# LayerNorm weight and bias for the next residual: applied in place by VectorE in pieces beside the next sublayer, instead of by GpSimd at the sublayer boundary

## The chip, the cores and the metric

The program runs on one core of one Trainium2 chip. The metric is device time of one execution in microseconds (us). The kernel before takes 1333.25 us as the median of three runs (1328.18 to 1336.28 us).

## The reference: what is computed

A decoder trunk of two layers over 256 tokens of width 1024, in float32. Each layer has three sublayers: a SwiGLU feed-forward (FFN), a mixer of four attention branches, and a second FFN. Every sublayer ends in the same way, and this is what the change touches:

```python
x = _layer_norm(DEEPNORM_ALPHA * x + (1 + gate) * F(x * (1 + scale) + shift), ln_g, ln_b)
# _layer_norm(r, g, b) = (r - mean) * rsqrt(var + eps) * g + b
```

The result x is needed twice. The next sublayer's matrix products need it modulated and transposed at once. The residual of the next sublayer needs it as plain rows, much later, at that sublayer's end.

## The kernel before, in words

Tokens lie in two tiles of 128 (t = 0, 1), the 1024 channels along the free axis. All products are made as three passes of exact parts (hi and lo of the weight, uh and ul of the input). A weight is loaded by SyncE's queue into one of five `raw` buffers (line 256), ScalarE rounds it to `hi` (line 259), VectorE makes `lo` = raw - hi (line 264), and only then is the `raw` buffer free for the next load. The six sublayers follow each other as FFN, mixer, FFN, FFN, mixer, FFN, so there are five boundaries between sublayers; the sixth ends the program through `store`.

**At a boundary** (`boundary`, lines 388 to 490), for each token tile: `resid` (lines 398 to 400) takes the products out of PSUM times the gate row G, adds ALPHA x, and gathers the statistics; `stats` (403 to 405) makes rstd, whose power is GpSimd's (405); `xhat` (413 or 415) normalizes the rows in four pieces of 256 columns; `norm` (423 to 434) transposes each piece on TensorE, scales and shifts it (429 on ScalarE or 431 on VectorE), and splits it into uh (433, ScalarE) and ul (434, VectorE). The LayerNorm weight and bias of the modulated input are folded into the column vectors gd and bd (383 to 385). Tile 0 goes through this while TensorE still makes the last products of the old sublayer; tile 1 goes through it in `finish`, behind the products of tile 0 in the new one.

**The rows for the next residual** are made in `rest` (480 to 488): four pairs on GpSimd, times the row g (486) and plus the row b (487), from the normalized rows `rt` into a new tile `x`. They are queued behind the boundary's last instructions on their engine.

**The rows g, b and G** of a sublayer come by GpSimd: a memset (345), a small load issued by GpSimd (346), and later a shuffle on VectorE that spreads the row over the partitions (352). Three buffers of the tag `row` hold them; a new row waits until the old row of its buffer is read. `sub_steps` says beside which of twelve steps of the sublayer each fetch is issued (ROW_G = 3, ROW_B = 4, GG = 4); the steps themselves are pairs of loads of adaLN weights and a multiply-and-sum on VectorE (304, 305).

**Order.** The program is written in one order with priorities, and a scheduler then orders each engine's queue by its own estimate of when things are ready; `high_priority` moves pieces ahead. In the mixer, `plan` lists which piece of attention follows which half pair of projections (a tick); `rope` (677 to 680) ends in an add on GpSimd (680) that the attention scores (875) wait for. In the FFN, `hidden(f)` is one pair of column tiles of the first product, and `post` (524 to 534) its activation; TensorE needs its PSUM bank back when VectorE has made `h` (527). The first two column tiles of an FFN are made per token tile, and `hT` (611) transposes their result, which waits for `h` (609).

Of the kernel before, what the change touches and what calls it, by code (L numbers as in the profile page):

```python
# [11 lines left out]
F32 = mybir.dt.float32  # L12
F32R = mybir.dt.float32r
BF16 = mybir.dt.bfloat16
AF = mybir.ActivationFunctionType
# [18 lines left out]
# columns of mix_w_in  # L34
# [5 lines left out]
# pairs of 128-column tiles whose products come out transposed  # L40
# [7 lines left out]
# offsets in the constants  # L48
C_COS, C_SIN, C_END = 0, 256, 512
# offsets in the constants of sums  # L50
R_ONE, R_SUF, R_FOX = 0, 128, 256
R_END = 256 + 640
# offsets in the masks
C_MC, C_MT, C_MA = 0, 384, 768
M_END = 768 + 1152
# depths of buffers, priorities and places of the pieces of work among each other
# [48 lines left out]
PJ = 5  # L105


def _consts():
# [5 lines left out]
    # minus sums of the first and of the second key tile, by columns (q0 k0, q1 k0, q1 k1)  # L114
# [27 lines left out]
def trunk(ctx: ExitStack, tc: tile.TileContext, x, xT, crow, ada0, adac, adab, w_in0, w_in0x, gcol, bcol, ln_g, ln_b,  # L142
# [46 lines left out]
    # 2 silu(c) = c * (1 + tanh(c / 2))  # L189
# [43 lines left out]
    held = {"ins": [], "left": 0, "free": 0}  # L233

    def behind():
        """queue what follows behind the boundary that has just been emitted, on its engines."""
        stack = ExitStack()
        for i in held["ins"]:
            stack.enter_context(tc.issue_after(i))
        return stack  # L240
# [4 lines left out]
    def load(*srcs):  # L245
        """srcs: [128, n] each; the parts of their halves, which are loaded in turns."""
# [32 lines left out]
    def split_mm(ps, w, xh, xl, start, stop, w_stationary=True):  # L279
        """ps += w^T x by three passes of exact parts."""  # L280
# [11 lines left out]
    mods = {(l, s): {} for l in range(DEPTH) for s in range(3)}  # L292

    def ada_cols(l, s, v):
        """steps that leave sum_k cond_k W_kn + b_n (+ 1) in columns [128, n // 128]."""
# [14 lines left out]
    def ada_gate(l, s):  # L310
        """steps that leave sum_k cond_k W_kn + b_n + 1 in every row of G."""
# [19 lines left out]
    def modulate(src, uh, ul, gd, bd, on_act):  # L331
        """parts of src * gd + bd; src may lie in PSUM."""
# [9 lines left out]
    def fetch_row(dst, row):  # L342
        """a row of DRAM into one partition of each 32; spread_row spreads it from there."""
# [16 lines left out]
    def sub_steps(l, s, nxt):  # L360
        """steps beside a sublayer's products: its gate and its LayerNorm's rows, the modulation of what follows."""
# [8 lines left out]
        for key, n, src in (("g", ROW_G, ln_g), ("b", ROW_B, ln_b)):  # L370
# [4 lines left out]
        seq = ada_cols(l, s, 2) + nx  # L375
        return [both(*before.get(n, []), f) for n, f in enumerate(seq)]

# [10 lines left out]
    def boundary(rt, accs, i, G, g, b, u, nxt):  # L388
        """rows: r = ALPHA x + G O, then LayerNorm; into u: its modulation for what follows."""
# [106 lines left out]
    def ffn(l, s, u, nxt, steps, first=False):  # L496
# [117 lines left out]
        for f in range(f0, NF):  # L614
            hidden(f)
            if first and f == F0 + SI:
                small_inputs()
# [562 lines left out]
```

## Time and profile before

| what | value |
|---|---|
| runs | 1328.18, 1333.25, 1336.28 us |
| profiled execution: its span, first to last instruction | 1336.7 us |
| TensorE busy | 1279.5 us (96%) |
| VectorE busy | 1045.9 us (78%) |
| ScalarE busy | 655.5 us (49%) |
| GpSimd busy | 193.0 us (14%) |
| read from HBM | 297.81 MB, 224 GB/s over the span |

The profile gives the profiled execution by its span alone; the span is 0.3% above the median of the three runs and 0.03% above the longest of them. The five boundaries lie near 207, 471, 671, 872 and 1134 us after the start. A row of the timeline gives start, duration, engine, line, operation, the tile written and the tiles read, and in brackets how long the engine was idle before it and which instruction ended that idle time.

### The profile page before, as it was taken

The page shows a single profiled execution, that of the slowest core. Times are in us where ns is not written, and L with a number is a line of the kernel's source. Part 1 is how long each engine was busy: PE and PEld are TensorE (multiplying, and loading weights), DVE is VectorE, ACT ScalarE, POOL GpSimd, SP SyncE. Part 2 cuts the span into 40 slices and gives each one's busy share as a digit, 9 for nine tenths or more (in the row PEclk, how much of TensorE's full clock was granted, in tenths as well). Part 3 has the DMA queues.
Part 4 walks back from the last instruction along what each step waited for, and adds up shares of the span by engine and source line. Part 5 has one row for each costly group of instructions (what it writes and reads, how often), then busy time and mean ns, then how long its engine had stood idle before and what let it go on. Part 6 is the DMA issues. An engine that isn't in the chain of part 4 may idle for free.

```text
span 1336.7 us, 23420 instructions
## 1 busy us (share of the span) xinstructions
PE 1279.5 (96%) x9178; PEld 1185.8 (89%) x9178; DVE 1045.9 (78%) x1661; ACT 655.5 (49%) x1023; POOL 193.0 (14%) x190
## 2 busy tenths in 40 slices
PE   6999998999999999999989999989999999899997
PEld 6989987899989889998979998988999998899996
DVE  7787888999855898876698876698997658986565
ACT  4644355457754445534345434354567544454440
POOL 0130004305011040000040000052060110400000
PEclk9999999999999989999999999989999999999999
DMA  9888992767755539877439877437677554596540
GB/s 340 317 294 317 314 312 95 254 193 254 254 177 188 190 132 319 307 265 248 149 138 315 301 266 243 140 126 248 201 252 242 189 190 158 174 328 199 184 142 32
DMA packets 85846, 300.41 MB, mean 225 GB/s; under 512 B 10604, under 2 KB 12316, under 8 KB 85736
## 3 DMA queue, kind: packets, MB, share of 16 engines
q1 hardware_dynamic: 84392, 298.00, 65.7%
q8 instruction: 72, 1.18, 0.3%
q10 hardware_dynamic: 576, 0.60, 0.1%
q0 software_dynamic: 768, 0.32, 0.1%
q14 instruction: 38, 0.31, 0.1%
HBM read 297.81 MB, written 1.07 MB: 224 GB/s over the span
## 4 chain that ended last, share of the span: by engine, by line
PE 57%; DMA 17%; DVE 16%; issue 5%; ACT 4%; POOL 1%; SPq 0%; DVEq 0%; ACTq 0%; POOLq 0%
PE mm L283 12%; PE mm L284 11%; PE mm L285 11%; DMA raw<-in_w_in_dram 10%; DVE lo L264 6%; DMA raw<-in_adac_dram 6%; PE acc L289 5%; PE acc L287 5%; PE acc L288 5%; DVE raw L305 2%; ACT hi L259 2%; DVE rt L415 2%; PE tp L283 1%; PE tp L284 1%; PE tp L285 1%
## 5 line engine op out<-in xcount | busy, mean ns | idle before, releaser
L264 DVE TENSOR_TENSOR lo<-raw,hi 128x1024 fp32r<-128x1024 f32 (+2 forms) x421 | 509.6, 1223 | 178.9 <-ACT hi L259 176.1
L259 ACT CAST hi<-raw 128x1024 fp32r<-128x1024 f32 (+1 forms) x422 | 434.6, 1040 | 354.6 <-PE mm L284 133.9
L283 PE MATMUL mm<-uh,hi 128*128 128x256 f32 x2032 | 576.8, 284 | 6.4 <-DVE h L527 5.4
L284 PE MATMUL mm<-ul,hi 128*128 128x256 f32 x2032 | 573.2, 282 | 0.0
L285 PE MATMUL mm<-uh,lo 128*128 128x256 f32 x2032 | 572.5, 282 | 0.3 <-DVE lo L264 0.3
L283 PEld LDWEIGHTS mm<-uh,hi 128*128 128x128 f32 x2032 | 385.0, 190 | 13.9 <-issue 6.3
L284 PEld LDWEIGHTS mm<-ul,hi 128*128 128x128 f32 x2032 | 385.1, 190 | 1.4
L285 PEld LDWEIGHTS mm<-uh,lo 128*128 128x128 f32 x2032 | 385.0, 190 | 0.8 <-DVE lo L264 0.5
L305 DVE CUSTOM_DVE_ANT_0 raw<-raw,cond_row,adab 128x1024 f32<-128x1024 f32 x128 | 164.1, 1292 | 43.2 <-DMA raw<-in_adac_dram 43.0
L287 PE MATMUL acc<-hi,hh 128*128 128x512 f32 x352 | 140.6, 399 | 1.7 <-ACT hh L533 1.6
L288 PE MATMUL acc<-lo,hh 128*128 128x512 f32 x352 | 139.1, 395 | 0.0
L289 PE MATMUL acc<-hi,hl 128*128 128x512 f32 x352 | 138.3, 396 | 0.4 <-POOL hl L534 0.4
L289 PEld LDWEIGHTS acc<-hi,hl 128*128 128x128 f32 x352 | 66.0, 188 | 17.8 <-DVE hl L534 1.2
L533 ACT CAST hh<-h 128x256 fp32r<-128x256 f32 x82 | 33.2, 405 | 98.7 <-DVE h L527 96.9
L287 PEld LDWEIGHTS acc<-hi,hh 128*128 128x128 f32 x352 | 66.1, 188 | 17.0 <-ACT hh L533 3.3
L405 POOL TENSOR_TENSOR rstd<-rstd,nhalf 128x1 f32<-128x1 f32 x12 | 7.6, 633 | 494.7 <-DVE rstd L404 494.7
L288 PEld LDWEIGHTS acc<-lo,hh 128*128 128x128 f32 x352 | 66.1, 188 | 13.9
L1065 POOL TENSOR_TENSOR merged<-merged,tg 128x512 f32<-128x512 f32 x16 | 23.0, 1451 | 143.8 <-DVE tg L1063 97.1
L289 PE MATMUL acc<-hi,ul 128*128 128x256 f32 (+1 forms) x128 | 41.3, 323 | 2.2 <-DVE ul L434 2.2
L287 PE MATMUL acc<-hi,uh 128*128 128x256 f32 (+1 forms) x128 | 41.7, 326 | 0.0
L534 DVE TENSOR_TENSOR hl<-h,hh 128x256 fp32r<-128x256 f32 x74 | 31.1, 420 | 12.6 <-ACT hh L533 12.6
L288 PE MATMUL acc<-lo,uh 128*128 128x256 f32 (+1 forms) x128 | 40.5, 316 | 0.0
(242 smaller groups left out, 1583.8 us busy)
## 6 DMA issues: line engine op xcount, KB each, us to landing
raw<-in_w_in_dram SPq DMA_DIRECT2D x174, 512.0 KB, 5.6
raw<-in_adac_dram SPq DMA_DIRECT2D x128, 512.0 KB, 5.4
raw<-in_mpair_dram SPq DMA_DIRECT2D x104, 512.0 KB, 5.1
raw<-in_w_out_dram SPq DMA_DIRECT2D x88, 512.0 KB, 5.4
ada<-in_ada_dram SPq DMA_DIRECT2D x16, 512.0 KB, 6.7
raw<-in_mwo_dram SPq DMA_DIRECT2D x16, 512.0 KB, 4.1
raw<-in_mv_dram SPq DMA_DIRECT2D x16, 384.0 KB, 3.5
raw<-in_mbr_dram SPq DMA_DIRECT2D x12, 512.0 KB, 3.9
```

The source lines that it names most:

```text
L259: nc.scalar.copy(hi[:, :half], raw[:, :half])
L264: held["lo"] = nc.vector.tensor_sub(lo[:, :half], raw[:, :half], hi[:, :half].bitcast(F32)).ins
L283: nc.tensor.matmul(ps, lhsT=wh, rhs=xh, start=start, stop=False)
L284: nc.tensor.matmul(ps, lhsT=wh, rhs=xl, start=False, stop=False)
L285: nc.tensor.matmul(ps, lhsT=wl, rhs=xh, start=False, stop=stop)
L287: nc.tensor.matmul(ps, lhsT=xh, rhs=wh, start=start, stop=False)
L288: nc.tensor.matmul(ps, lhsT=xh, rhs=wl, start=False, stop=False)
L289: return nc.tensor.matmul(ps, lhsT=xl, rhs=wh, start=False, stop=stop).ins
L305: nc.vector.tensor_tensor_reduce(raw, raw, cond_row, 0.5, adab_sb[:, l * 3 + s, v, n:n + 1], ALU.mult, ALU.add, accum_out=t[:, n:n + 1])
L415: nc.vector.tensor_scalar(rt[:, t, hs], rt[:, t, hs], mv[t][:, 0:1], rstd[t], op0=ALU.subtract, op1=ALU.mult)
L533: nc.scalar.copy(hh, h)
L534: eng.tensor_sub(hl, h, hh.bitcast(F32))
```

## The change

`rest` goes. The residual sum is now written into the tile x itself (line 399 before, 402 now), xhat, transposes and `store` work on x, and no new tile is made. The weight and bias are applied to x in place by VectorE, by `affine(t, h)`, in four pieces of two instructions (lines 485 and 486 now), one piece for each token tile and half of the columns. The pieces are handed to the next sublayer: an FFN emits one after each `hidden(f)` from f = 3 on, a mixer emits them at ticks 42 to 45. In the mixer the rows g and b are fetched at step 10 instead of 3 and 4, and two empty steps are added so that their spreading still comes three steps later. Constants, comments and line numbers apart, this is the diff:

```diff
+AFF = 3
+AM = 42
+ROW_M = 10
...
-        for key, n, src in (("g", ROW_G, ln_g), ("b", ROW_B, ln_b)):
+        for key, n, src in (("g", ROW_M if s == 1 else ROW_G, ln_g), ("b", ROW_M if s == 1 else ROW_B, ln_b)):
...
-        seq = ada_cols(l, s, 2) + nx
+        seq = ada_cols(l, s, 2) + nx + ([lambda: None] * (ROW_M + GD + 1 - 12) if s == 1 else [])
...
-            nc.vector.scalar_tensor_tensor(rt[:, t, c], xt[t][:, c], ALPHA, rt[:, t, c], op0=ALU.mult, op1=ALU.add)
-            nc.vector.bn_stats(st6[:, 2 * t + h], rt[:, t, c])
+            nc.vector.scalar_tensor_tensor(xt[t][:, c], xt[t][:, c], ALPHA, rt[:, t, c], op0=ALU.mult, op1=ALU.add)
+            nc.vector.bn_stats(st6[:, 2 * t + h], xt[t][:, c])
...
-                nc.vector.tensor_scalar(rt[:, t, hs], rt[:, t, hs], mv[t][:, 0:1], rstd[t], op0=ALU.subtract, op1=ALU.mult)
+                nc.vector.tensor_scalar(xt[t][:, hs], xt[t][:, hs], mv[t][:, 0:1], rstd[t], op0=ALU.subtract, op1=ALU.mult)
...
-            rest()
-
-        def rest():
-            with behind():
-                for t in range(2):
-                    xn = ap_.tile([P, D], F32, tag=f"x{t}", bufs=1, name=f"x{t}")
-                    for h in range(2):
-                        hs = slice(h * 512, (h + 1) * 512)
-                        nc.gpsimd.tensor_tensor(xn[:, hs], rt[:, t, hs], g[:, hs], op=ALU.mult)
-                        nc.gpsimd.tensor_tensor(xn[:, hs], xn[:, hs], b[:, hs], op=ALU.add)
-                    xt[t] = xn
...
+        def affine(t, h):
+            hs = slice(h * 512, (h + 1) * 512)
+            nc.vector.tensor_tensor(xt[t][:, hs], xt[t][:, hs], g[:, hs], op=ALU.mult)
+            nc.vector.tensor_tensor(xt[t][:, hs], xt[t][:, hs], b[:, hs], op=ALU.add)
+
+        held.update(finish=finish, first=last["pe", 0], affine=[lambda t=t, h=h: affine(t, h) for t in range(2) for h in range(2)])
...
             hidden(f)
+            if not first and f >= AFF and held["affine"]:
+                held["affine"].pop(0)()
...
+            for n, piece in enumerate(held["affine"]):
+                on(AM + n, piece)
```

The scheduler has the last word on where the pieces stand. **VectorE at the first boundary**, from tile 1's last residual sum to its four xhat; x_108 and x_109 are the rows of token tiles 0 and 1. Before:

```order
L434 TENSOR_TENSOR ul<-utmp,uh 128x2x128
L398 TENSOR_TENSOR rt<-acc,G 128x512
L434 TENSOR_TENSOR ul<-utmp,uh 128x2x128
L399 SCALAR_TENSOR_TENSOR rt<-x_109,rt 128x512
L434 TENSOR_TENSOR ul<-utmp,uh 128x2x128
L400 BN_STATS st_2246<-rt 128x6
L403 BN_AGGR mvar<-st_2246 128x2
L404 TENSOR_SCALAR rstd<-mvar 128x1
L415 TENSOR_SCALAR rt<-rt,mvar,rstd 128x256 x4
```

The same stretch of VectorE's queue in the changed kernel, where L485 is the multiply by g and L486 the add of b:

```order
L437 TENSOR_TENSOR ul<-utmp,uh 128x2x128
L486 TENSOR_TENSOR x_108<-x_108,b 128x512
L401 TENSOR_TENSOR rt<-acc,G 128x512
L437 TENSOR_TENSOR ul<-utmp,uh 128x2x128
L402 SCALAR_TENSOR_TENSOR x_109<-x_109,rt 128x512
L437 TENSOR_TENSOR ul<-utmp,uh 128x2x128
L403 BN_STATS st_2246<-x_109 128x6
L485 TENSOR_TENSOR x_108<-x_108,g 128x512
L406 BN_AGGR mvar<-st_2246 128x2
L486 TENSOR_TENSOR x_108<-x_108,b 128x512
L407 TENSOR_SCALAR rstd<-mvar 128x1
L418 TENSOR_SCALAR x_109<-x_109,mvar,rstd 128x256 x4
```

The first piece's multiply stands a little ahead of these rows, behind tile 1's first BN_STATS. So tile 0's two pieces, four instructions, have moved ahead of tile 1's rstd and xhat; this is so at all five boundaries. Of tile 1's two pieces the first multiply stands right behind the boundary's last L437, ahead of six of the next sublayer's lo, and the other three instructions among its first products.

**GpSimd at the same boundary**, into the mixer. Before:

```order
L405 TENSOR_TENSOR rstd<-rstd,nhalf 128x1
L486 TENSOR_TENSOR x_2408<-rt,g 128x512 x2
L487 TENSOR_TENSOR x_2408<-x_2408,b 128x512 x2
L486 TENSOR_TENSOR x_2413<-rt,g 128x512 x2
L487 TENSOR_TENSOR x_2413<-x_2413,b 128x512 x2
L345 MEMSET b 128x1024
L345 MEMSET G 128x1024
L346 DMA b<-in_ln_b_dram 4x1024
L680 TENSOR_TENSOR qa<-qa,t_2508 128x256
L680 TENSOR_TENSOR qa<-qa,t_2515 128x256
L680 TENSOR_TENSOR qa<-qa,t_2583 128x256
```

And in the changed kernel:

```order
L408 TENSOR_TENSOR rstd<-rstd,nhalf 128x1
L680 TENSOR_TENSOR qa<-qa,t_2498 128x256
L680 TENSOR_TENSOR qa<-qa,t_2505 128x256
L348 MEMSET g 128x1024
L348 MEMSET b 128x1024
L349 DMA g<-in_ln_g_dram 4x1024
L349 DMA b<-in_ln_b_dram 4x1024
L680 TENSOR_TENSOR qa<-qa,t_2573 128x256
```

The eight instructions of `rest` are gone, and the fetch of g and b has moved in between two of the rope's adds. In an FFN the eight are gone too, and the fetch of g stays where it was.

**VectorE late in layer 0's second FFN**, at the last adaLN step of that FFN. Before:

```order
L525 SCALAR_TENSOR_TENSOR th<-th,mm 128x256
L305 ISA raw,scale<-raw,cond_row,adab 128x1024
L305 ISA scale 128x1
L264 TENSOR_TENSOR lo<-raw,hi 128x1024
L383 TENSOR_TENSOR gd<-gcol,scale 128x8
L384 TENSOR_TENSOR bd<-bcol,scale 128x8
L527 SCALAR_TENSOR_TENSOR h<-th,mm 128x256
```

And in the changed kernel:

```order
L523 SCALAR_TENSOR_TENSOR th<-th,mm 128x256
L308 ISA raw,scale<-raw,cond_row,adab 128x1024
L308 ISA scale 128x1
L525 SCALAR_TENSOR_TENSOR h<-th,mm 128x256
L386 TENSOR_TENSOR gd<-gcol,scale 128x8
L387 TENSOR_TENSOR bd<-bcol,scale 128x8
L267 TENSOR_TENSOR lo<-raw,hi 128x1024
```

Here h has moved ahead of a lo and of the two small products; at the same place of the next FFN the order stays as before. SyncE's queue, which issues the weight loads, is the same row for row.

## Rows read from the trace of the kernel before

**Rows 1.** The page, part 1: busy time, share of the span, instructions.

```profile
PE 1279.5 (96%) x9178; PEld 1185.8 (89%) x9178; DVE 1045.9 (78%) x1661; ACT 655.5 (49%) x1023; POOL 193.0 (14%) x190
```

**Rows 2.** The page, part 4: the chain that ended last, by engine.

```profile
PE 57%; DMA 17%; DVE 16%; issue 5%; ACT 4%; POOL 1%; SPq 0%; DVEq 0%; ACTq 0%; POOLq 0%
```

**Rows 3.** Busy time by stretch: the five boundaries, and one FFN between them.

```profile
core 0: us, PE busy (x) PEld busy (x) DVE busy (x) ACT busy (x) POOL busy (x), PEclk, DMA share, GB/s
206.70:222.40 15.70, 12.00 (x58) 10.16 (x57) 14.91 (x21) 7.56 (x17) 13.95 (x13) 0.89 0.01 2
470.50:489.00 18.50, 15.97 (x108) 14.73 (x107) 17.62 (x26) 9.08 (x18) 15.22 (x14) 0.82 0.07 19
669.00:688.00 19.00, 15.30 (x117) 13.76 (x116) 18.13 (x28) 10.39 (x21) 15.21 (x14) 1.00 0.02 6
870.00:888.00 18.00, 14.60 (x70) 12.61 (x69) 17.01 (x25) 9.73 (x21) 14.91 (x14) 0.81 0.01 2
1133.50:1151.50 18.00, 14.98 (x107) 13.90 (x106) 17.12 (x25) 9.46 (x18) 15.19 (x14) 0.91 0.05 12
...
495.00:665.00 170.00, 167.39 (x1159) 155.36 (x1158) 130.24 (x187) 76.30 (x103) 1.13 (x2) 0.99 0.77 265
```

**Rows 4.** VectorE in order of time at the first boundary.

```profile
202.47 0.73 DVE L415 TENSOR_SCALAR rt<-rt,mvar,rstd 128x256 f32<-128x256 f32 x2
...
205.68 0.43 DVE L434 TENSOR_TENSOR ul<-utmp,uh 128x256 fp32r<-128x256 f32 x1
...
206.94 0.69 DVE L398 TENSOR_TENSOR rt<-acc,G 128x512 f32<-128x512 f32 x1
207.54 0.41 DVE L434 TENSOR_TENSOR ul<-utmp,uh 128x256 fp32r<-128x256 f32 x1
...
210.61 5.18 DVE L415 TENSOR_SCALAR rt<-rt,mvar,rstd 128x256 f32<-128x256 f32 x4 [0.68 <-POOL rstd L405]
...
216.75 1.88 DVE L434 TENSOR_TENSOR ul<-utmp,uh 128x256 fp32r<-128x256 f32 x2
...
221.43 5.75 DVE L264 TENSOR_TENSOR lo<-raw,hi 128x1024 fp32r<-128x1024 f32 x5
```

**Rows 5.** GpSimd in order of time there: the first and last of `rest`.

```profile
210.55 2.54 POOL L486 TENSOR_TENSOR x<-rt,g 128x512 f32<-128x512 f32 x2
...
218.31 2.92 POOL L487 TENSOR_TENSOR x<-x,b 128x512 f32<-128x512 f32 x2
```

**Rows 6.** TensorE in order of time: tile 1's first ul product, first and second boundary.

```profile
217.26 0.69 PE L289 MATMUL acc<-hi,ul 128*128 128x384 f32 x1 [0.23 <-DVE ul L434]
...
481.32 0.58 PE L289 MATMUL acc<-hi,ul 128*128 128x256 f32 x1 [0.30 <-DVE ul L434]
```

**Rows 7.** VectorE and ScalarE in order of time at the second boundary.

```profile
474.61 5.23 DVE L415 TENSOR_SCALAR rt<-rt,mvar,rstd 128x256 f32<-128x256 f32 x4 [0.69 <-POOL rstd L405]
...
477.36 0.41 ACT L433 CAST uh<-utmp 128x256 fp32r<-128x256 f32 x1
...
485.46 5.82 DVE L264 TENSOR_TENSOR lo<-raw,hi 128x1024 fp32r<-128x1024 f32 x5
```

**Rows 8.** Groups by line and shape: a VectorE sum of two SBUF tiles of 128x512.

```profile
L1065 DVE TENSOR_TENSOR merged<-merged,tg 128x512 f32<-128x512 f32 x8 | 5.5, 687 | 0.2
```

**Rows 9.** Late in layer 0's second FFN: TensorE's waits (engine, line waited for, us), then VectorE.

```profile
PE mm L283 <- DVE h L527: 2.3, 1, 2.3
...
609.64 1.22 DVE L264 TENSOR_TENSOR lo<-raw,hi 128x1024 fp32r<-128x1024 f32 x1
...
610.93 0.42 DVE L527 SCALAR_TENSOR_TENSOR h<-th,mm 128x256 f32<-128x256 f32 x1
```

**Rows 10.** GpSimd's rope adds, and TensorE's wait for one, first mixer.

```profile
234.29 0.72 POOL L680 TENSOR_TENSOR qa<-qa,t 128x256 f32<-128x256 f32 x1 [10.69 <-DVE t L679]
235.29 1.43 POOL L680 TENSOR_TENSOR qa<-qa,t 128x256 f32<-128x256 f32 x1 [0.28 <-DVE t L679]
...
247.97 0.49 PE L875 MATMUL acc<-ka,qa 64*128 64x128 f32 x4 [0.81 <-POOL ka L680]
```

More of the change, by code (lines that the diff above doesn't have):

```diff
@@ L412, in xhat @@
                     nc.vector.tensor_scalar(sums[:, t:t + 1], mv[t][:, 0:1], rstd[t], -1.0, op0=ALU.mult, op1=ALU.mult)
-                nc.scalar.activation(rt[:, t, hs], rt[:, t, hs], AF.Identity, bias=sums[:, t:t + 1], scale=rstd[t])
+                nc.scalar.activation(xt[t][:, hs], xt[t][:, hs], AF.Identity, bias=sums[:, t:t + 1], scale=rstd[t])
             else:
-                nc.vector.tensor_scalar(rt[:, t, hs], rt[:, t, hs], mv[t][:, 0:1], rstd[t], op0=ALU.subtract, op1=ALU.mult)
+                nc.vector.tensor_scalar(xt[t][:, hs], xt[t][:, hs], mv[t][:, 0:1], rstd[t], op0=ALU.subtract, op1=ALU.mult)
         def norm(t, q, on_act, gate):
@@ L423, in norm @@
                     last["pe", t] = nc.tensor.transpose(ps[:, j * 128:(j + 1) * 128],
-                                                        rt[:, t, (kt + j) * 128:(kt + j + 1) * 128], ident).ins
+                                                        xt[t][:, (kt + j) * 128:(kt + j + 1) * 128], ident).ins
             tmp = sp.tile([P, 2, 128], F32, tag="tmp", bufs=4, name="utmp")
@@ L438, in store @@
         def store(t):
-            xn = ap_.tile([P, D], F32, tag=f"x{t}", bufs=1, name=f"x{t}")
+            xn = xt[t]
             for h in range(2):
                 hs = slice(h * 512, (h + 1) * 512)
-                nc.vector.scalar_tensor_tensor(xn[:, hs], rt[:, t, hs], mv[t][:, 0:1], g[:, hs], op0=ALU.subtract, op1=ALU.mult)
+                nc.vector.scalar_tensor_tensor(xn[:, hs], xn[:, hs], mv[t][:, 0:1], g[:, hs], op0=ALU.subtract, op1=ALU.mult)
             for n, w in ((0, 512), (512, 512)) if t == 0 else ((0, 512), (512, 256), (768, 256)):
@@ L477, in finish @@
             held["ins"] = [*last["ad"], last["pow"], last["pe", 1]]
-            rest()
-        def rest():
-            with behind():
-                for t in range(2):
-                    xn = ap_.tile([P, D], F32, tag=f"x{t}", bufs=1, name=f"x{t}")
-                    for h in range(2):
-                        hs = slice(h * 512, (h + 1) * 512)
-                        nc.gpsimd.tensor_tensor(xn[:, hs], rt[:, t, hs], g[:, hs], op=ALU.mult)
-                        nc.gpsimd.tensor_tensor(xn[:, hs], xn[:, hs], b[:, hs], op=ALU.add)
-                    xt[t] = xn
-        held.update(finish=finish, first=last["pe", 0])
+        def affine(t, h):
[3 more added lines that the diff above has]
+        held.update(finish=finish, first=last["pe", 0], affine=[lambda t=t, h=h: affine(t, h) for t in range(2) for h in range(2)])
     TAIL = ((0, 0, 512), (0, 512, 512), (1, 0, 512), (1, 512, 512))
```

## The prediction

> **What bounds the kernel now.** I read the busy shares first. TensorE is busy 96% of the span and GpSimd 14% [rows 1], so an instruction taken off GpSimd is worth nothing by itself. Next is the chain that ended last: TensorE has 57% of it and GpSimd 1%, but VectorE has 16% [rows 2], so there are places where TensorE waits for VectorE. The table by stretch shows where. In an FFN between boundaries TensorE is busy 167.39 of 170 us; in the five boundaries it is busy 12.00 of 15.70, 15.97 of 18.50, 15.30 of 19.00, 14.60 of 18.00 and 14.98 of 18.00 us [rows 3]. That is 3.70 + 2.53 + 3.70 + 3.40 + 3.02 = 16.4 us without a product. [...] So the change is worth what it does to five bubbles.
>
> The order of time at the first boundary shows what fills them. Tile 0's two xhat on VectorE take 0.73 us together, 0.37 each; tile 1's four, the same instruction on the same shape, take 5.18, 1.30 each [rows 4]. GpSimd's multiply and add start at 210.55, and two of them take 2.54, 1.27 each; the last pair ends at 221.23 [rows 5]. So while `rest` runs, each xhat lasts as long as one GpSimd instruction. ul is slowed as well: 0.43 for one at 205.68, 1.88 for two at 216.75 [rows 4]. At the second boundary the four xhat take 5.23 [rows 7]. The reader is to see that TensorE waits behind these: its first product with tile 1's ul starts at 217.26 and 481.32, with a wait for ul in both rows [rows 6], which is 6.65 and 6.71 us after the first xhat [rows 4, 7].
>
> **The change part by part.**
>
> *Removed: `rest` on GpSimd, 40 instructions.* What counts is the path from the first xhat of tile 1 to the first ul product, 6.7 us now. Undisturbed it is not in the trace; two rows bound it. Tile 0's same path took from 202.47 to 205.68 + 0.43, that is 3.6 us [rows 4], with other VectorE work in between: the upper end. At the second boundary uh was ready at 477.36 + 0.41, 3.16 us after the first xhat [rows 7]; less 0.93, by which that one xhat was slow, and with 0.43 for ul, it is 2.7: the lower end. I take 3.2, the middle. Saving: 6.7 - 3.2 = 3.5 us a boundary (3.1 to 4.0).
>
> *Added: 40 VectorE sums of 128x512.* One such sum of two SBUF tiles takes 0.69 us [rows 8], 27.5 us in all. Half of them would be harmless if they stood where the change's words put them; the scheduler's order has tile 0's four instructions ahead of tile 1's rstd at every boundary, so xhat itself starts later. Independent VectorE instructions start 0.60 apart behind one of 128x512 (206.94 to 207.54) [rows 4]. The inserted ones also part instructions that need each other's result and so fill some time that was empty; I take 0.5 each, 2.0 us a boundary. Ends: 0.69 each, 2.75; and 0.3 each, 1.2, if half of it lies in waits of VectorE. Net: 3.5 - 2.0 = 1.5 us a boundary, **7.5 us for five** (0.4 to 2.8 each, 2 to 14).
>
> *The other 20* stand among the next sublayer's lo. The lo begin 10.85 us after the first xhat at the second boundary (485.46 - 474.61) [rows 7]. Two parts of that are the slow xhat (5.23 - 1.46 = 3.8 us) and the slow ul (about 0.5 each, 2.0 for four); with xhat 2.0 later, lo would still start over 3 us sooner, against 0.69 for the one multiply ahead of it. The raw buffers come free, and the loads restart, that much sooner. So I cost these at nothing in the FFNs. Should that cover go, their price is 4 x 0.69 = 2.75 us a sublayer.
>
> *The mixers.* GpSimd's fetch of g and b now waits for the last piece, and four of the rope's adds are queued behind it. TensorE's first attention product waits for the last of these adds already, 0.81 us at 247.97, 11 us after the second add has ended at 236.72 [rows 10]; that distance hides the fetch. But VectorE has the pieces between the rope's parts there, and TensorE comes earlier. I charge 0.5 us to each of two mixers, **-1.0**. Ends: nothing, and one collision of an add with a VectorE instruction, 1.4 each: the add took 1.43 where the one before it took 0.72 [rows 10]. [...]
>
> The two spreads of g and b in each mixer move to a later stretch. No row has one; the nearest VectorE instruction of 128x1024 is lo with 1.15 (5.75 / 5) [rows 4]. VectorE is idle 22% of the span [rows 1], and there I hide them; without that cover it is 2.3 us a mixer.
>
> *The row fetch in the FFNs.* A memset and a load of g still stand ahead of rstd's power on GpSimd, behind the last read of G. VectorE's path to rstd is now 2 us longer and hides them better. b's memset waits for the pieces, and only b's load and G's are queued behind it, which are needed at the sublayer's end: nothing.
>
> *The clock.* [...] I take **2 us**; ends 10 saved, and 1.7 lost by a spell of 3.5 us at the third boundary, which has none now.
>
> *Late in layer 0's second FFN* TensorE waits 2.3 us for h [rows 9]. h now stands ahead of the lo that started at 609.64; before, it started at 610.93. That is **1.3 us** sooner (0 to 2.3).
>
> The start before the first boundary and the end are the same work.
>
> **Sum.** 7.5 + 2 + 1.3 - 1.0 = 9.8, say 10 us less than the profiled execution's 1336.7 us. That span is 1.0026 times the median of the runs, 1333.25, and what lies around it is not shown, so I scale: 1326.7 / 1.0026 = **1323 us**. All ends together, the covers held, reach from 3 us lost (2 - 1.7 - 2.8) to 26 gained.
>
> **Rivals.** About 1% is what a measurement of this kernel can tell from no change: 13 us.
>
> A. *The early pieces are nearly free and the clock stays up.* If the four instructions lie in waits (1.2 us), the boundary gives 2.8 x 5 = 14; with half of the clock's 10 and the 1.3 it is 20 us: 1336.7 - 20 = 1316.7, scaled 1313. For it: four of the five clock columns are between 0.81 and 0.91 [rows 3]. Against it: at the first boundary VectorE is busy 14.91 of 15.70 us, so little waiting is there to be filled. Chance 0.25.
>
> B. *The gain is handed on to the next wait.* TensorE comes earlier to products whose lo, h or loads are no earlier. VectorE is busy 130.24 of the FFN's 170 us and gets 2.75 more [rows 3, 8]; if each sublayer takes back all but 0.6 us, 3 us remain: 1330. Against it: the lo move ahead too. Chance 0.13.
>
> C. *The moved sums collide with the rope's adds,* at 1.4 us a mixer and some more behind them, so that 7 us remain: 1326. For it: 1.43 against 0.72 [rows 10]. [...] Against it: the wait at 247.97 comes 11 us after. Chance 0.06.
>
> D. *Slower: xhat is not slow because of GpSimd.* If the four xhat keep their 5.2 us for a reason of their own (their place in memory, their place behind the power), nothing is saved, and 2.0 us a boundary of early pieces are lost: 5 x 2.0 + 1.0 - 1.3 = 10 more, 1346 or scaled 1343. It decides where the four take longer than 5.2 - 2.0 = 3.2 us. Against it: 0.37 for tile 0's, behind the same power, and the match of 1.30 with 1.27 [rows 4, 5]. Chance 0.06.
>
> That the change does not do what it says is half true and in the sum: tile 0's pieces stand in the boundary, not beside the next sublayer.
>
> **Chances and range.** My forecast has 0.50. Faster by over 1% (under 1320): nearly all of A and the upper part of the forecast's spread, 0.34. Slower by over 1%: D, 0.06. Within 1%: 0.60. The range of 1312 to 1335 takes in B, C, the forecast's ends for clock and pieces, and the half of A above 1312; it leaves out D and A's far end.
>
> **What would show it.** After the change the four xhat of tile 1 should take about 1.5 us at each boundary, ul 0.4 each, and the power should come about 2 us later after tile 1's last residual product than now. The first ul product should start 3 to 3.5 us after the first xhat instead of 6.7. TensorE's idle time in the five boundaries should fall from 16.4 to about 9 us, and the wait for h of 2.3 us to about 1. It is wrong if xhat stays above 0.8 us each (D), if the pieces lie in waits (the power comes no later: A), or if new waits for hT, lo or the rope's add of more than 1 us stand behind each boundary (B, C).

## The result, and the profile after

The changed kernel takes 1318.62 us (median of four runs, 1318.43 to 1320.82), the kernel before beside it 1330.78 us (four runs, 1328.18 to 1336.28). The ratio is 0.9888, with a 95% interval of 0.9861 to 0.9915: faster by 1.1%. The forecast was 1323 us, with a range of 1312 to 1335. A later set of runs gave 1322.92 us (1313.05 to 1323.43) against 1334.22 us, ratio 0.9903 (0.9871 to 0.9935).

The profiled execution of the changed kernel has a span of 1319.0 us; its run took 1320.82 us. Against the profiled execution before it is 17.7 us shorter, more than the 12.2 us between the medians: that execution of the kernel before was a long one. First the page's busy times and its chain by engine, which answer to [rows 1, 2].

```profile
PE 1271.0 (96%) x9178; PEld 1180.2 (89%) x9178; DVE 1036.8 (79%) x1701; ACT 653.7 (50%) x1023; POOL 134.2 (10%) x150
...
PE 41%; issue 26%; DVE 13%; DMA 12%; ACT 4%; POOL 3%; DVEq 0%; ACTq 0%; SPq 0%; POOLq 0%
```

VectorE's share of the chain fell from 16% to 13%. GpSimd lost 59 us of work, and VectorE is 9 us less busy than before, although it has 40 instructions more: they add 28 us, and its other instructions give back 37, xhat 19 of it and ul 13. TensorE is busy 8.5 us less for the same 9178 instructions, so they ran faster. The busy time by stretch at the five boundaries answers to [rows 3]; the columns are the same.

```profile
206.70:219.00 12.30, 10.12 (x57) 8.89 (x56) 11.55 (x29) 7.48 (x18) 1.51 (x2) 1.00 0.00 1
464.00:483.00 19.00, 17.96 (x127) 15.96 (x126) 18.06 (x42) 11.11 (x25) 2.74 (x4) 1.00 0.01 2
661.00:678.00 17.00, 16.00 (x127) 15.09 (x126) 16.07 (x35) 10.81 (x23) 2.13 (x3) 1.00 0.12 35
853.00:871.00 18.00, 15.75 (x88) 14.41 (x87) 16.79 (x34) 12.15 (x25) 1.50 (x2) 0.91 0.17 52
1114.00:1131.00 17.00, 16.02 (x116) 14.25 (x115) 16.14 (x40) 10.35 (x24) 2.73 (x4) 1.00 0.01 2
```

The reader is to take two things from these rows. Length minus TensorE's busy time is 2.18, 1.04, 1.00, 2.25 and 0.98 us, 7.45 us in all where it was 16.4 (counted over the same products; 7.43 in the profiled execution of the later set). And the clock column, which stood at 0.89, 0.82, 1.00, 0.81 and 0.91, is 1.00 everywhere but at the fourth boundary. Such a column is the mean of two levels, as narrow windows show: at the first boundary before, 0.50 inside one spell and 1.00 behind it.

```profile
216.90:219.20 2.30, 2.07 (x7) 1.94 (x7) 2.30 (x4) 1.20 (x4) 2.30 (x3) 0.50 0.03 7
219.50:222.00 2.50, 2.50 (x15) 2.26 (x14) 2.50 (x3) 2.50 (x3) 2.50 (x3) 1.00 0.00 0
```

Products of one shape start 0.32 us apart in the first window and 0.17 apart in the second:

```profile
218.71 0.52 PE L287 MATMUL acc<-hi,uh 128*128 128x384 f32 x1
219.02 0.52 PE L288 MATMUL acc<-lo,uh 128*128 128x384 f32 x1
...
220.09 0.34 PE L287 MATMUL acc<-hi,uh 128*128 128x384 f32 x1
220.26 0.34 PE L288 MATMUL acc<-lo,uh 128*128 128x384 f32 x1
```

So 2 x (1 - clock) x length is the time at 0.50, called half clock here: 3.5, 6.7, 0, 6.8 and 3.2 us before, 20 us in all, and 2 x 0.09 x 18 = 3.2 us now, where narrow windows show 0.50 from 862.9 to 865.6.

VectorE in order of time at the first boundary, which answers to [rows 4]:

```profile
208.47 0.68 DVE L401 TENSOR_TENSOR rt<-acc,G 128x512 f32<-128x512 f32 x1
...
210.94 0.68 DVE L485 TENSOR_TENSOR x<-x,g 128x512 f32<-128x512 f32 x1
...
211.66 0.69 DVE L486 TENSOR_TENSOR x<-x,b 128x512 f32<-128x512 f32 x1
...
213.09 1.38 DVE L418 TENSOR_SCALAR x<-x,mvar,rstd 128x256 f32<-128x256 f32 x4 [0.67 <-POOL rstd L408]
...
215.51 0.43 DVE L437 TENSOR_TENSOR ul<-utmp,uh 128x256 fp32r<-128x256 f32 x1
...
217.78 5.76 DVE L267 TENSOR_TENSOR lo<-raw,hi 128x1024 fp32r<-128x1024 f32 x5
```

At the second boundary, VectorE and then TensorE, which answers to [rows 6, 7]:

```profile
475.48 1.38 DVE L418 TENSOR_SCALAR x<-x,mvar,rstd 128x256 f32<-128x256 f32 x4 [0.69 <-POOL rstd L408]
...
480.90 5.76 DVE L267 TENSOR_TENSOR lo<-raw,hi 128x1024 fp32r<-128x1024 f32 x5
```

```profile
478.35 0.38 PE L292 MATMUL acc<-hi,ul 128*128 128x256 f32 x1
```

At the first boundary tile 1's four xhat take 1.38 us where they took 5.18, but they begin 4.62 us after the start of tile 1's last residual product (208.47 to 213.09), where it was 3.67 (206.94 to 210.61): two of the inserted instructions stand in between. TensorE at the first boundary, waits in brackets, which answers to [rows 6]:

```profile
213.55 0.44 PE L426 MATMUL mm<-ident,x 128*128 128x128 f32 x2 [1.61 <-DVE x L418]
215.53 0.44 PE L290 MATMUL acc<-hi,uh 128*128 128x384 f32 x1 [0.57 <-ACT uh L436]
...
215.99 0.44 PE L292 MATMUL acc<-hi,ul 128*128 128x384 f32 x1
```

The first product with tile 1's ul starts 2.90 us after the first xhat, without a wait for ul; before, 6.65. At the second boundary it is 478.35 - 475.48 = 2.87 us, before 6.71.

**Where the 17.7 us lie.** TensorE issues the same number of instructions in the same stages, so the start of the n-th one in both traces shows the lead grow and shrink. The five boundaries, each with the first products behind it, gain 4.3, 3.6, 4.4, 2.7 and 2.9 us, 17.9 together. The late stretch of the FFNs between the boundaries, where TensorE waits for h [rows 9], gains 3.4 and 4.0. The two mixers lose 2.6 and 4.2. The program's start loses 0.8. That is 17.9 + 7.4 - 6.8 - 0.8 = 17.7. Within the first mixer the loss is 5.6 us up to branch D's softmax; 3.0 come back behind it, at a place where the execution before has TensorE waiting 2.17 us for a VectorE result and a spell at half clock behind that (0.50 from 383.4 to 386.6).

Two places inside the first mixer show its loss. VectorE, then TensorE, at the rope, which answers to [rows 10]:

```profile
231.59 0.68 DVE L485 TENSOR_TENSOR x<-x,g 128x512 f32<-128x512 f32 x1
232.30 1.11 DVE L486 TENSOR_TENSOR x<-x,b 128x512 f32<-128x512 f32 x1
```

```profile
244.32 0.49 PE L875 MATMUL acc<-ka,qa 64*128 64x128 f32 x4 [0.72 <-POOL ka L680]
246.15 0.49 PE L875 MATMUL acc<-ka,qa 64*128 64x128 f32 x4 [1.34 <-POOL ka L680]
```

The last piece stands among the rope's parts, its add beside a GpSimd add and 1.11 us long, and TensorE waits 2.06 us for ka instead of 0.81. VectorE, then TensorE, 90 us later, where the weights p of branch D are made (L789 to L795):

```profile
334.03 0.01 DVE L355 LOAD_MASK_SELECT G<-G  x1 [4.71 <-DMA G<-gflat]
334.03 1.33 DVE L355 STREAM_SHUFFLE G<-G 128x1024 f32<-128x1024 f32 x1
...
339.29 0.17 DVE L792 RECIPROCAL su<-su 128x2 f32<-128x2 f32 x1 [0.15 <-ACT p L791]
```

```profile
338.42 0.33 PE L749 MATMUL tp<-ident,p 128*128 128x128 f32 x1 [0.49 <-ACT p L795]
339.94 0.33 PE L749 MATMUL tp<-ident,p 128*128 128x128 f32 x1 [0.69 <-ACT p L795]
```

Before, the spread of g stood ahead of this softmax, that of b inside it, and the spread of G behind its reciprocals:

```profile
334.26 1.36 DVE L352 STREAM_SHUFFLE b<-b 128x1024 f32<-128x1024 f32 x1
335.52 0.20 DVE L792 RECIPROCAL su<-su 128x2 f32<-128x2 f32 x2
...
335.65 1.32 DVE L352 STREAM_SHUFFLE G<-G 128x1024 f32<-128x1024 f32 x1
```

Now G's spread stands first, stops VectorE's queue for 4.71 us until its load lands, and the softmax stands behind it. In the second mixer the same wait is 5.01 us.

### The profile page after: what moved, and what is told of

The parts are those of the page before. It is cut to its first block, busy times and chain, and to the rows that moved or that the text cites. A ratio compares the mean times of both kernels' runs of the same rounds, so it can differ in the third digit from the quotient of the medians.

```text
span 1319.0 us, 23422 instructions
## 1 busy us (share of the span) xinstructions
PE 1271.0 (96%) x9178; PEld 1180.2 (89%) x9178; DVE 1036.8 (79%) x1701; ACT 653.7 (50%) x1023; POOL 134.2 (10%) x150
## 4 chain that ended last, share of the span: by engine, by line
PE 41%; issue 26%; DVE 13%; DMA 12%; ACT 4%; POOL 3%; DVEq 0%; ACTq 0%; SPq 0%; POOLq 0%
PE mm L286 8%; PE mm L287 8%; PE mm L288 8%; DMA raw<-in_w_in_dram 7%; DVE lo L267 5%; PE acc L292 3%; PE acc L290 3%; PE acc L291 3%; ACT hi L262 2%; POOL lb L968 2%; DVE raw L308 2%; DMA raw<-in_adac_dram 1%; PE tp L286 1%; PE tp L287 1%; PE tp L288 1%
## 5 line engine op out<-in xcount | busy, mean ns | idle before, releaser
L267 DVE TENSOR_TENSOR lo<-raw,hi 128x1024 fp32r<-128x1024 f32 (+2 forms) x421 | 507.7, 1220 | 165.4 <-ACT hi L262 163.7
L290 PEld LDWEIGHTS acc<-hi,hh 128*128 128x128 f32 x352 | 66.1, 188 | 16.8 <-ACT hh L531 2.8
L522 ACT ACTIVATE th<-mm 128x256 f32<-128x256 f32 x74 | 27.9, 377 | 24.8 <-PE mm L288 24.7
```

Source lines behind the costliest of these rows:

```text
L267: held["lo"] = nc.vector.tensor_sub(lo[:, :half], raw[:, :half], hi[:, :half].bitcast(F32)).ins
L290: nc.tensor.matmul(ps, lhsT=xh, rhs=wh, start=start, stop=False)
L522: nc.scalar.activation(th, pg, AF.Tanh, scale=0.5)
```

## The experiments

All times are medians; ratios are to the kernel before, run beside them on the same chip, with a 95% interval.

### GpSimd at the boundary again, in place

```diff
+            for t in range(2):
+                for h in range(2):
+                    affine(t, h)
...
+            with behind():
...
+                nc.gpsimd.tensor_tensor(xt[t][:, hs], xt[t][:, hs], g[:, hs], op=ALU.mult)
+                nc.gpsimd.tensor_tensor(xt[t][:, hs], xt[t][:, hs], b[:, hs], op=ALU.add)
...
```

> Only the rewriting in place is kept; GpSimd applies g and b at the boundary again and the mixer's rows are fetched at steps 3 and 4 as before. Theory (the 5.2 us of the four xhat are GpSimd's multiplies and adds beside them): xhat back at 1.3 us each, the first ul product 6.5 to 6.7 us after the first xhat, and the time of before, 1331 us (1327 to 1336). Rival (xhat was slow for a reason that the in-place rewriting removed, such as where rt and x lie): xhat 0.35 to 0.4 us each though GpSimd works, and 1318 to 1322 us.

Measured: 1334.2 us, ratio 1.0013 (0.9989 to 1.0037), as the theory said. VectorE, then GpSimd, at the first boundary:

```profile
208.39 5.18 DVE L418 TENSOR_SCALAR x<-x,mvar,rstd 128x256 f32<-128x256 f32 x4 [0.68 <-POOL rstd L408]
213.49 1.27 DVE L434 TENSOR_SCALAR utmp<-tp,gd,bd 128x128 f32<-128x128 f32 x3
214.68 1.84 DVE L437 TENSOR_TENSOR ul<-utmp,uh 128x256 fp32r<-128x256 f32 x2
```

```profile
208.34 2.54 POOL L488 TENSOR_TENSOR x<-x,g 128x512 f32<-128x512 f32 x2
```

xhat is back at 1.30 us each. Working in place is worth nothing by itself, and the whole gain comes from what GpSimd no longer does there.

### All pieces late

```diff
+            with tc.issue_after(held["lo"]):
                 nc.vector.tensor_tensor(xt[t][:, hs], xt[t][:, hs], g[:, hs], op=ALU.mult)
                 nc.vector.tensor_tensor(xt[t][:, hs], xt[t][:, hs], b[:, hs], op=ALU.add)
```

> The changed kernel with all pieces of g and b queued behind the last lo that has been emitted, so none stands ahead of tile 1's rstd. Theory (the four early instructions delay tile 1's xhat by 2.0 us a boundary): the power comes about 2 us sooner after tile 1's last residual product, and TensorE gets what its waits there allow: they are 1.05, 0.92 and 0.98 us at the second, third and fifth boundary and 2.2 us at the first and fourth, so 7 us, with the half-clock spell at 863 us another 1.7: 1310 to 1312 us. Rival 1 (the early pieces lie in waits of VectorE): xhat no sooner, 1317 to 1320 us. Rival 2 (handed on: lo, rope adds and loads are no earlier): waits at the boundaries gone but new ones behind them, 1315 to 1320 us.

Measured: 1321.11 us, ratio 0.9905 (0.9876 to 0.9933). TensorE's idle time over five boundary windows (the sum row: length, then TensorE's busy time), and two of its waits:

```profile
sum 78.00, PE 76.22 PEld 68.90 DVE 67.43 ACT 51.70 POOL 10.58; mean PE 15.24 PEld 13.78 DVE 13.49 ACT 10.34 POOL 2.12
```

```profile
524.65 0.51 PE L292 MATMUL acc<-hi,hl 128*128 128x512 f32 x1 [2.15 <-DVE hl L532]
...
1176.60 0.79 PE L292 MATMUL acc<-hi,hl 128*128 128x512 f32 x1 [3.06 <-DVE hl L532]
```

The time is not the theory's 1310 to 1312 us. The boundaries keep 1.78 us of idle time instead of 7.45, so the early pieces cost 5.7 us there, 1.1 a boundary (1.3 into a mixer, 1.0 into an FFN). But the second rival holds: in the FFNs VectorE comes late with hl, for up to 3.06 us, and nothing remains of the gain.

### The same, with GpSimd making the late pieces of the FFNs

```diff
+        def affine(t, h, eng=nc.vector, gate=None):
...
+                held["affine"].pop(0)(nc.gpsimd, nc.gpsimd.tensor_scalar(late, hs_[f][1].bitcast(F32)[:, 0:1], 0.5, None, op0=ALU.mult).ins)
...
```

> As the one with all pieces late, but in the three FFNs GpSimd makes them, one after each of the column tiles 3 to 6, each behind a small GpSimd multiply that waits for hl of that tile. It tells the place from the engine. Theory (the place was the cost, since no xhat stands beside them there): a VectorE instruction beside one of the 24 GpSimd instructions takes up to 1.3 us longer, which VectorE's 22% of idle time hides; within 2 us of the kernel with late VectorE pieces. Rival (GpSimd is costly wherever it runs): lo of 1.2 us take 2.4, hi and the raw buffers come later, TensorE waits for mm behind column tiles 3 to 6 and the time is 5 us or more above it.

Measured: 1320.27 us, ratio 0.989 (0.986 to 0.9921). Groups by line: lo, and the GpSimd multiplies by g and adds of b (busy time, mean ns of one):

```profile
L267 DVE TENSOR_TENSOR lo<-raw,hi 128x1024 fp32r<-128x1024 f32 (+2 forms) x421 | 520.4, 1252 | 165.4 <-ACT hi L262 163.8
...
L486 POOL TENSOR_TENSOR x<-x,b 128x512 f32<-128x512 f32 x12 | 26.2, 2180 | 0.9
L485 POOL TENSOR_TENSOR x<-x,g 128x512 f32<-128x512 f32 x12 | 22.5, 1877 | 0.0
```

It is within 2 us of the kernel with late VectorE pieces: away from the boundary the engine decides little. The rival was right on the single lo, which takes up to 2.3 us beside such an instruction, but only 14 more of the 421 than in the changed kernel last over 1.7 us: all lo together are longer by 520.4 - 507.7 = 12.7 us than in the changed kernel. A GpSimd instruction takes 1.9 to 2.2 us on the average there; the first ones at the boundary took 1.27.

### Without the 40 instructions

```diff
-        held.update(finish=finish, first=last["pe", 0], affine=[lambda t=t, h=h: affine(t, h) for t in range(2) for h in range(2)])
+        held.update(finish=finish, first=last["pe", 0], affine=[])
```

> The changed kernel without the 40 VectorE instructions: the LayerNorm weight and bias of the rows for the next residual are left out, so its time tells what the instructions cost in all. With all pieces late the boundaries' waits fell from 7.4 to 1.8 us, but waits for hl of 7.7 us came up in the FFNs. Theory (the pieces cost as much in the FFNs as at the boundary, because VectorE has no room there): without them both go, the boundaries keep about 1.8 us of waits, no wait for hl over 1 us, and the time is 1318.6 - 5.6 - 1.7 (a half-clock spell at the fourth boundary) = 1311 us (1309 to 1313). Rival (late pieces are free, the waits for hl are chance, and early ones too): 1316 to 1320 us.

Measured: 1310.35 us, ratio 0.981 (0.9754 to 0.9866). The boundaries keep 1.5 us of idle time, and no wait for hl is over 0.3 us. Against the changed kernel's first set the 40 instructions cost 1318.6 - 1310.4 = 8.2 us of the time (10 by the two ratios; the sets were not run side by side) for 28 us of VectorE's: neither where the changed kernel has them nor all late are they free. The last experiment shows that this is a matter of their places.

### Longer waits, without GpSimd

```diff
+                for q in range(8):
+                    c = slice(q % 4 * 256, q % 4 * 256 + 256)
+                    nc.vector.tensor_scalar(rt[:, 0, c], rt[:, 0, c], mv[1][:, 0:1], rstd[1], op0=ALU.subtract, op1=ALU.mult)
                 for q in range(4):
                     xhat(1, q)
```

> The changed kernel with eight more VectorE instructions of the form of xhat (128x256, 0.33 us each, on rows that nobody reads any more) between tile 1's rstd and its xhat at each of the five boundaries: tile 1 comes 2.6 us later, and TensorE's waits there grow from 7.4 to about 20 us in all, a little more than before the change. It tells whether the half-clock spells follow the waits. Theory (they do; before the change they cost 15 us of which the boundaries had 10): mean clock falls from 0.995 to 0.987 to 0.990, 1318.6 + 13 + 8 = 1340 us (1336 to 1343). Rival (the spells were GpSimd's or chance): mean clock stays at 0.994 to 0.997 and the time is 1318.6 + 13 = 1331.6 us (1329 to 1333).

Measured: 1336.0 us, ratio 1.0006 (0.9979 to 1.0032), mean clock 0.983 to 0.987: the theory, at the lower end of its time and a little below its clock. The five boundaries by stretch, then VectorE at the second:

```profile
206.70:226.00 19.30, 14.60 (x73) 13.72 (x73) 17.35 (x38) 10.31 (x21) 1.52 (x2) 0.82 0.15 44
470.00:492.00 22.00, 18.68 (x138) 17.52 (x138) 20.85 (x45) 12.02 (x25) 2.17 (x3) 0.92 0.14 40
663.00:686.00 23.00, 19.67 (x126) 18.03 (x125) 21.11 (x49) 12.80 (x26) 2.70 (x4) 0.85 0.06 21
862.00:884.00 22.00, 17.40 (x87) 15.92 (x86) 20.64 (x45) 12.46 (x27) 1.51 (x2) 0.84 0.12 33
1125.00:1147.00 22.00, 18.74 (x110) 16.53 (x109) 20.70 (x49) 10.12 (x24) 2.74 (x4) 0.85 0.02 3
```

```profile
478.39 2.68 DVE L478 TENSOR_SCALAR rt<-rt,mvar,rstd 128x256 f32<-128x256 f32 x8 [0.69 <-POOL rstd L408]
480.98 1.38 DVE L418 TENSOR_SCALAR x<-x,mvar,rstd 128x256 f32<-128x256 f32 x4
```

The idle time is 19.2 us in all, and the clock falls at every boundary: 2 x (1 - clock) x length gives 6.9, 3.5, 6.9, 7.0 and 6.6 us, 31 us at half clock, which counted at half is 15.5 us lost. Xhat is as fast as in the changed kernel and GpSimd has no more to do, so waits made by VectorE alone, 3.3 to 4.7 us a boundary here, are followed by the lower clock: it did not take GpSimd's work beside them.

### G's spread later in the mixers

```diff
-        before.setdefault(GG + GD, []).append(lambda: spread_row(st["G"]))
+        before.setdefault(GG + GD + (2 if s == 1 else 0), []).append(lambda: spread_row(st["G"]))
```

> The changed kernel with one edit: in the mixers VectorE's spread of G over the partitions is issued two steps later. In the trace of the changed kernel this spread stops VectorE's queue for 4.7 and 5.0 us until G's load lands, D's softmax stands behind it, TensorE waits 1.5 and 2.0 us for p, and each is followed by a half-clock spell of 3.4 us. Theory (the order of the spreads is what costs the mixers): those waits go (3.5 us) and with them the two spells (2 x 1.7): 1318.6 - 6.9 = 1311.7 us (1310 to 1314). Rival (the softmax waits for something else, the sums of the forget gates that GpSimd prepares): waits for p remain at over 1 us and the time is 1317 to 1320 us.

Measured: 1317.85 us, ratio 0.9881 (0.9857 to 0.9904): the rival's time, not 1311.7, and not to be told from the changed kernel's 0.9888. VectorE, then TensorE, in the first mixer:

```profile
337.93 1.28 DVE L308 CUSTOM_DVE_ANT_0 raw<-raw,cond_row,adab 128x1024 f32<-128x1024 f32 x1 [3.80 <-DMA raw<-in_adac_dram]
...
339.14 0.16 DVE L792 RECIPROCAL su<-su 128x2 f32<-128x2 f32 x1
```

```profile
339.79 0.33 PE L749 MATMUL tp<-ident,p 128*128 128x128 f32 x1 [2.10 <-ACT p L795]
```

G's spread no longer stops the queue here, but the next in line does: an adaLN multiply waits 3.80 us for its load, with the softmax's second reciprocal behind it. In the second mixer the waits for p are gone. The rival's reason, GpSimd's sums, is not what the trace shows. The theory was half right on the wait: the order of the queue makes it, but one of two blockers was named. That the wait costs the time is not shown.

### Both blockers moved, with GpSimd's late pieces

The edit of G's spread, and in the mixers

```diff
+            held["su"] = nc.vector.reciprocal(su, su).ins
...
+                with tc.issue_after(held["su"]) if (s, v, c) == (2, 1, 0) else ExitStack():
                     nc.vector.tensor_tensor_reduce(raw, raw, cond_row, 0.5, adab_sb[:, l * 3 + s, v, n:n + 1],
```

> Pieces late, by GpSimd in the FFNs and VectorE in the mixers, and two edits in the mixers: G's spread two steps later, and the first adaLN multiply of the next scale behind the last reciprocal of a softmax, since with G's spread moved alone the second reciprocal of D stood behind that multiply's load (3.8 us) and TensorE still waited 2.1 us for p. Theory (the mixers' loss is the order of VectorE's queue): no wait for p over 0.5 us in either mixer, no half-clock spell there, boundaries' waits about 2 us: 1320.3 - 4 - 2 = 1314 us (1311 to 1316). Rival (another instruction stands in the way then, and the gain is handed on again): 1318 to 1321 us.

Measured: 1317.55 us, ratio 0.9872 (0.9827 to 0.9918). No wait for D's p is left and no spell of half clock before the program's end (mean clock 0.998), but waits of 1.34 and 1.10 us for the next branch's pt, and of 1.73, 1.46 and 1.47 us for h in the FFNs, are. It lies between theory and rival.

### Pieces late in the mixers alone

```diff
+            with tc.issue_after(held["lo"]) if nxt[1] == 1 else ExitStack():
                 nc.vector.tensor_tensor(xt[t][:, hs], xt[t][:, hs], g[:, hs], op=ALU.mult)
...
```

First with both edits of the mixers' order, beside the kernel above:

> The changed kernel with pieces behind the last lo in the mixers alone (VectorE's in the FFNs stay where the scheduler had them), and the two edits of the mixers' order: G's spread two steps later, the adaLN multiply of the next scale behind the softmax's last reciprocal. Theory (early pieces cost 2.2 us of TensorE's waits at each boundary into a mixer, first and fourth, of which late ones leave 0.9; in the FFNs they are best left early): waits of the first and fourth boundary 0.9 us each instead of 2.2, no spell of half clock at the fourth, no wait for p over 0.5 us: 1317.9 - 2.6 - 1.7 - 2 = 1311.6 us (1309 to 1314). Rival (handed on to the rope's adds or the loads): 1316 to 1319 us.

Measured: 1310.11 us (1306.5 to 1314.31), ratio 0.9816 (0.9768 to 0.9865), mean clock 0.995 to 0.998, within the theory's range. It has all 40 instructions and is as fast as the kernel without them beside it (1310.35 us): with the pieces late in the mixers and early in the FFNs, no cost of theirs shows. Then without the two edits, and the changed kernel and the best one again, on one chip:

> The changed kernel with the pieces late in the mixers and nothing else edited: the part of the last kernel (1310.1 us) that concerns the boundary, without the two edits of VectorE's order in the mixers. Theory (the early pieces at the first and fourth boundary cost 2.6 us of waits and a half-clock spell of 1.7; the waits for p with their spells stay): 1318.6 - 4.3 = 1314.3 us (1312 to 1316). Rival (the 8.5 us came from the mixers' order alone): 1317 to 1320 us.

> The changed kernel as it is, beside the others on one chip: 1318.6 us (1316 to 1321), mean clock 0.994 to 0.997.

> The kernel with late pieces in the mixers and both edits of the mixers' order once more, to compare it with the changed kernel on one chip. If its 1310.1 us are its own: 1308 to 1312 us and 0.991 to 0.996 of the changed kernel's time, mean clock 0.996 to 0.998. If they were the chip's: within 3 us of the changed kernel.

Measured: 1313.55 us (1310.63 to 1317.28), ratio 0.985 (0.9824 to 0.9877), with late pieces alone; 1322.92 us, ratio 0.9903 (0.9871 to 0.9935), for the changed kernel; 1313.07 us (1308.38 to 1313.76), ratio 0.9835 (0.9809 to 0.9861), for the best one. The first came out as its theory said; the changed kernel lies above its 1316 to 1321 us, and the best one above its 1308 to 1312 us, though at 0.9926 of the changed kernel's time. By the medians late pieces in two mixers are worth 9.4 us: five of the changed kernel's six runs lie above all six with late pieces. Against its first set (1318.62 us), which was not run beside these, it is 5. The two edits of order cannot be told from nothing beside them. TensorE's waits at the first boundary and the rope, with late pieces alone:

```profile
213.90 0.44 PE L426 MATMUL mm<-ident,x 128*128 128x128 f32 x2 [0.54 <-DVE x L418]
215.90 0.44 PE L290 MATMUL acc<-hi,uh 128*128 128x384 f32 x1 [0.39 <-ACT uh L436]
...
245.35 0.49 PE L875 MATMUL acc<-ka,qa 64*128 64x128 f32 x4 [0.81 <-POOL ka L680]
```

At the boundary 0.93 us remain of 2.18, at the rope 0.81 of 2.06. In the changed kernel's trace of that set (mean clock 0.992) the clock fell at the rope and at D's softmax in both mixers, four times 3.4 us; with late pieces (0.997) it fell at neither. G's spread was not moved here, and in the first mixer it found its load landed:

```profile
329.07 1.35 DVE L355 STREAM_SHUFFLE G<-G 128x1024 f32<-128x1024 f32 x1
```

In the second mixer it waited 4.90 us, as in the changed kernel. This version beats both kernels in its set.

## Why the prediction was right, and where it was wrong

The time came out 4.4 us below the forecast, inside the range, and xhat's part of the mechanism is shown; but that it came so near is in part luck: two terms of the sum were off by 6 us each in the profiled pair, in opposite directions, the clock and the mixers.

**`rest` removed: right.** The path from first xhat to first ul product was to shorten by 3.5 us (3.1 to 4.0); it shortened by 3.75 and 3.84 (6.65 to 2.90, 6.71 to 2.87). Not all of that is TensorE's: with `rest` gone and no early pieces (all pieces late) its idle time fell from 16.4 to 1.78 us, 2.9 a boundary, where I took 3.5. GpSimd's work put back brings xhat back to 5.18 us, so rival D is refuted, not only unlikely.

**The 20 early instructions: the size.** I took 2.0 us a boundary. At the first boundary the power comes 0.94 us later, 3.08 us after tile 1's last residual product before (206.94 to 210.02) and 4.02 now (208.47 to 212.49):

```profile
210.02 0.55 POOL L405 TENSOR_TENSOR rstd<-rstd,nhalf 128x1 f32<-128x1 f32 x1 [0.47 <-DVE rstd L404]
```

```profile
212.49 0.56 POOL L408 TENSOR_TENSOR rstd<-rstd,nhalf 128x1 f32<-128x1 f32 x1 [2.32 <-DVE rstd L407]
```

At the five boundaries it is 0.55 to 1.66 us later, and TensorE loses 1.1 us a boundary, just under my lower end of 1.2. I counted all four, but only two (at the second and fifth boundary three) stand behind tile 1's last residual product; the others filled time in which VectorE was not yet on the path. So the net of the boundaries was not 17.5 - 10 = 7.5 but 14.6 - 5.7 = 8.9 us of idle time: both sizes were too large, and the errors nearly cancel.

**The other 20, at nothing: held in the FFNs, as far as shown.** I named lo that start 3 us sooner as their cover, and they do (at the second boundary 5.42 us behind the first xhat, 475.48 to 480.90, where it was 10.85). In the mixers, which I charged apart, a piece stands among the rope's parts, on the way to ka.

**The clock: the step that failed most.** I took 2 us, with 10 as the far end. No run shows the 2; in its place the boundaries of the profiled pair show 20 us at half clock before and 3.2 after, which counted at half is 10 - 1.6 = 8.4 us. By the start of the products, 0.32 us apart instead of 0.17, a little under half of such a time is lost: the 16.8 us are then about 8. Over all runs the mean clock was 0.984 to 0.992 before and 0.992 to 0.997 after; (1 - clock) x span is 14 to 16 us lost on the average of each set of runs before, and 6 and 9 us after. The stall experiment shows that the clock follows the waits: with 3.3 to 4.7 us without a product at a boundary it fell at all five. In the kernel before, no wait for xhat was over 1.14 us, but 2.5 to 3.7 us without a product lay together, and it fell at four of five. In the changed kernel it fell behind the wait of 1.69 us at the fourth boundary, but not behind that of 1.61 at the first, nor behind 1.70 at the first in the later set; and in the profiled execution at none of the boundaries into an FFN, whose idle time is 1.0 us in all. At the boundaries, halving the waits took away nearly all of the spells, not half of them; in the mixers new ones came up.

**The mixers: wrong.** I charged 0.5 us each, 1.0 in all, for the rope, and hid the two moved spreads. The profiled pair shows 6.8. The step that failed is the charge for pieces beside the rope and the boundary into the mixer: late pieces alone took the rope's wait from 2.06 back to 0.81 us and the time down by 9.4 us in its set. The spreads of g and b were indeed hidden where they went. What I missed in the queue is the third one: with g and b gone, G's spread stood ahead of the softmax and waited for its load. I had asked what the moved instructions cost at their new place, not who moves up at the old one. What that costs stays open: moving G's spread showed another blocker behind it, moving both gained nothing beside late pieces, and whether G's spread waits at all in its place differs with the landing of its load (4.71 us in the changed kernel's first mixer, nothing there with late pieces). Rival B, the gain handed on to the next wait, is what happened in the mixers.

**Late h: the term held on the average; the rest is that execution's.** I credited 1.3 us in layer 0's second FFN, where h moved ahead of a lo. The wait fell from 2.31 to 0.71 us:

```profile
605.05 0.39 PE L286 MATMUL mm<-uh,hi 128*128 128x256 f32 x1 [0.71 <-DVE h L525]
```

But it fell from 2.34 to 0.96 in the next FFN too, where the order at that place had not changed. And the kernel with GpSimd at the boundary, no faster than before and with lo ahead of h as before, waits only 0.54 us (1.31 in the next FFN):

```profile
605.49 0.39 PE L286 MATMUL mm<-uh,hi 128*128 128x256 f32 x1 [0.54 <-DVE h L528]
```

Of the thirteen traces, six have lo ahead of h at this place and seven h ahead of lo. The six wait 0.5 to 2.9 us there, 1.7 on the average, the seven 0 to 0.9 us, 0.5 on the average. That is 1.2 us, near the 1.3, though these kernels differ in other things too. The rest of the 7.4 us is not the change's as far as is shown: on the same execution before, the kernel with GpSimd at the boundary gains 3.6 and 3.7 us in these two stretches, where the changed kernel gains 3.4 and 4.0.

**Rival A** was the nearest to what happened: the clock stayed up, and the early pieces were cheaper than I took them. Its sum leaves out the mixers' 1.0, and its 1313 us are what the kernel reaches once the pieces are late in the mixers (1313.55 and 1313.07 us). **Rival C**, a collision with the rope's adds, came near its price: TensorE's wait at the first mixer's rope grew by 1.25 us where it priced 1.4. But only 0.42 us of that is a collision (the add of b took 1.11 us instead of 0.69); the rest is that the two sums stand in VectorE's queue there.

## What to carry to other kernels

When an instruction leaves a queue, look at who moves up into its place: an instruction that used to arrive late enough for its load may now stop the queue in front of work that is ready, as G's spread did for 4.71 us. Elementwise work on GpSimd that makes VectorE's instructions on the path longer, as here each xhat 1.30 instead of 0.35 us, is worth moving away from them. Where it goes is to be tried stage by stage: into the mixers, with their tight chain at the rope, late pieces were better (1313.55 against 1322.92 us), while all pieces late, in the FFNs too, took 1321.11 us (ratio 0.9905 against 0.985), though early ones cost 1.0 us of idle time at each boundary into an FFN. Count a shortened wait of TensorE once for the time and once for the clock it keeps: at the five boundaries here 8.9 us of idle time and about 8 by the clock.

## What the runs showed of the hardware

A GpSimd multiply or add of 128x512 took 1.27 to 1.46 us beside VectorE at the first boundary. Each xhat beside it took 1.30 instead of 0.35, and with GpSimd put back at the boundary each ul 0.92 instead of 0.43, while utmp took 1.27 us for three there, as in the stall kernel without GpSimd (1.26). xhat and ul read SBUF and utmp reads PSUM; that this is what tells them apart is not shown, since no run changes it alone. Both engines pay: beside the lo of the FFNs a GpSimd instruction took 1.9 to 2.2 us on the average, and a lo up to 2.3 instead of 1.2 (1252 ns instead of 1220 on the average of all 421).

What G's spread pays for standing first in its queue is the time to its load's landing: it waited 4.71 and 5.01 us in one execution of the changed kernel, and in the kernel with GpSimd's late pieces not at all. GpSimd, whose issue of G's load waits for the store ahead of it to land, waited 1.59 us for that store in the first mixer there, in the changed kernel 4.19 and 4.49.
